# A list scheduler's clock for VectorE and GpSimd: one price more, and another order of layer 0

## The chip, the cores and the metric

The kernel runs on one core of a Trainium2 chip. The metric is the device time of one execution in microseconds (us); the median of several runs counts. The core has TensorE (PE; its weight loads are shown apart, as PEld), VectorE (DVE), ScalarE (ACT), GpSimd (POOL) and the DMA queues, of which SyncE (SP) issues most.

## The reference, cut to what matters

One inference step of a two-layer decoder, for a prompt of 256 tokens and 8 samples of one token (264 columns, T), all in float32:

```python
for i in range(DEPTH):                      # layer 0, layer 1
    h = rmsnorm(x, norm_mix[i])
    if i % 2 == 0:
        proj = h @ w_in_a[j]
        o_rwkv, sh, S = rwkv7_mix(proj[..., :RWKV_PROJ], ...)
        o_s5, hr, hi = s5_mix(proj[..., RWKV_PROJ:], ...)   # a scan over time, then y * sigmoid(y @ w_glu + b_glu)
        mix = jnp.concatenate([o_rwkv, o_s5], -1) @ w_out_a[j]
    else:
        proj = h @ w_in_c[j]
        mix, S = retention_mix(proj, st_ret[j], pos, ret_gn[j], w_out_c[j])
    x = x + mix.astype(x.dtype)
    h = rmsnorm(x, norm_ffn[i])
    x = x + swiglu(h, ffn_w_gate[i], ffn_w_up[i], ffn_w_down[i])
y = rmsnorm(x, norm_final)
```

Outputs are y of both groups and the final states of all mixers.

## The kernel before, in words

**The weight stream.** Every weight matrix is read in pieces of 512 rows by 256 columns (`raw`). A *granule* is half of one: 512 rows (4 tiles of 128) by 128 output columns. For each granule ScalarE rounds the weights to a short format (`wh`) and VectorE takes the rest (`wl<-raw,wh`, 128x512): `split_to` (L469), two granules ahead of their use. TensorE then does 12 matmuls, wh by xh, wh by xl and wl by xh for each of the 4 tiles. `run_stream` (L554) walks over all granules in a fixed order of tasks: the input projection of layer 0 (`w_in_a`, granules 0 to 135), the S5 gate (`s5_w_glu`, from granule 136), the output projection, the FFN, and the same for layer 1.

**The side work.** RWKV, S5, the samples and the evacuations of accumulators are generators whose operations are not issued at once but recorded (`issue`, L291) with what they depend on. Between two half granules `pump` (L518) issues recorded operations whose time, by the builder's own clocks, has come. A task that needs a flag (`need`, L549) forces side operations, earliest time first, until the flag is there: an input tile needs a free row buffer, the S5 gate needs the flag "s5".

**The clocks.** `emit` (L259) issues one instruction. It prices it with `cost` (L214), takes the larger of the engine's clock and the time its operands are ready (`after`, L241), and adds the price to the engine's clock `clk` ("P", "V", "S", "G", "D" for TensorE, VectorE, ScalarE, GpSimd and DMA). All choices, which recorded operation goes next and on which of two engines a copy or a square goes, are made by these clocks while the program is built. The finished program is a fixed order on each engine; on the chip the engines wait for each other by semaphores only. All instructions are issued through `emit`, so that nearly all have one line in the profile, L281 (L287 loads ScalarE's function tables).

**The chain of S5** (`s5`, L1145): GpSimd and VectorE prepare parameters, then a recurrence of 64 steps, each of three VectorE operations:

```python
            self.mul(t, bc(h[:, None], [128, 2, 2, 32]), w)
            self.add(o, o, t[:, 0])
            self.add(o, o, t[:, 1, ::-1])
```

In the profile these are `ar_tmp<-t,ar_tmp 128x128` and two `t<-t,ar_tmp 128x64`. After it comes `s5_out` (L1233), in two halves of eight rounds, one with its products on VectorE, one on GpSimd; each round's last matmuls and its copy `ar_tmp<-ps 128x164` wait for the recurrence. Then follow GELU (`128x1312`), a rearranging copy, and the flag "s5", behind which the gate's granules stand. The squares of the first norm (`first_squares`, L619) may go to ScalarE or GpSimd, their sums to VectorE or GpSimd.

Of the kernel before, what the change touches and what calls it, by code (L numbers as in the profile page):

```python
# [14 lines left out]
PSUM = bass.MemoryType.PSUM  # L15
# [45 lines left out]
class Task:  # L61
    def __init__(self, w, row0, nk, c0, rhs, done, need=None):
        self.w, self.row0, self.nk, self.c0 = w, row0, nk, c0
        self.rhs, self.done, self.need, self.pre = rhs, done, need, None
# [64 lines left out]
class Builder:  # L129
    def __init__(self, ctx, tc, ins, outs, dumps=None):  # L130
        self.ctx, self.tc, self.nc = ctx, tc, tc.nc
        self.I, self.O, self.C0 = ins, outs, ins["cst"]
        self.dumps = dumps or {}
        self.side, self.rec = [], None
        self.evac = Side(None, -1)
        self.clk = dict.fromkeys("PVSGD", 0.0)
        self.where, self.uses, self.pend = {}, {}, {}
        self.tick, self.cols, self.warm = 0, 0.0, False
        self.flags = Flags(self)
        self.act_set = None  # L140
        nc = self.nc
        self.V, self.G, self.S, self.P = (Eng(self, e, k) for e, k in
                                          ((nc.vector, "V"), (nc.gpsimd, "G"), (nc.scalar, "S"), (nc.tensor, "P")))
        self.Q, self.QG, self.QS = (Eng(self, e, "D") for e in (nc.sync, nc.gpsimd, nc.scalar))
        pool = lambda name, **k: ctx.enter_context(tc.tile_pool(name=name, **k))
        self.pw = pool("pw", bufs=1)
        self.pc = pool("pc", bufs=1)
        self.pb = pool("pb", bufs=1)
        self.ps = pool("ps", bufs=1, space=PSUM)
        ctx.enter_context(tc.manual_schedule())  # L150
        self.banks = [self.ps.tile([128, 512], F32, name=f"ps{i}", tag=f"ps{i}") for i in range(8)]
        self.layer, self.held = 0, {}
        self.turn, self.bank, self.open, self.busy = 0, {}, [], [None] * 4
        for b in self.banks:
            self.cells(b)
# [103 lines left out]
    def emit(self, eng, name, a, k):  # L259

        a = [self.real(x) for x in a]
        key, uses = eng.key, self.operands(name, a, k)
        c = self.cost(key, name, a)
        t = self.after(key, uses)
        if key == "D":
            one = a[1].ap[0][1] == 1 and a[0].shape[0] > 1
            t = self.clk["D"] = max(t + (7.5 if one else 1.7), self.clk["D"]) + c
        else:
            if key == "P":
                while self.clk["P"] + 0.1 >= (self.tick + 1) * 3.4133:  # L270
                    self.warm = self.cols >= 3277
                    self.tick, self.cols = self.tick + 1, 0.0
                n = int(np.prod(a[0].shape[1:]))
                self.cols += n * (1 if a[1].dtype == F32R else 2 if name == "transpose" else 4) * a[1].shape[0] / 128
                c *= 1 if self.warm else 2
            elif key == "S":
                self.functions(ACT_SET.get(a[2]))
            t = self.clk[key] = max(self.clk[key], t) + c
        for n, (at, bits), w in uses:
            self.uses[n][0 if w else 1, "PVSG".index(key) if key != "D" else 3][at] = t  # L280
        getattr(eng.eng, name)(*a, **k)  # L281
        return t
# [1546 lines left out]
```

## Time and profile before

| | |
|---|---|
| Median of 3 runs | 3126.82 us (3126.31 to 3127.84) |
| Profiled execution | 3128.85 us, span 3127.1 us |
| Granted TensorE clock, mean | 0.985 |
| Busy: PE, PEld, DVE, ACT, POOL | 3052.4, 2940.0, 1970.2, 1542.6, 333.9 us |
| Instructions of DVE, ACT, POOL | 3728, 2913, 527 |

The span is the time from the first to the last instruction of the profiled execution. A group of the profile is named by what it writes and reads (`wl<-raw,wh`) and its shape in partitions and elements. `ps` are the PSUM banks, `ar_...` the areas of layer 0, `t` the area that holds x and the S5 states. The records of two instructions in a row on one engine overlap by some 0.1 us.

### The profile page before, as it was taken

How to read it: one execution, taken by the hardware profiler on the slowest of the kernel's cores; microseconds unless marked ns; L12 is line 12 of the kernel's file. 1: busy time of each engine (PE TensorE's matmuls, PEld its weight loads, DVE VectorE, ACT ScalarE, POOL GpSimd, SP SyncE). 2: the span in 40 equal slices, each digit the busy share in tenths (PEclk: the TensorE clock that was granted, in tenths of full speed). 3: DMA queues.
4: the chain of work that ended last, by engine and by line, in shares of the span. 5: the costliest groups of instructions: out<-in, count | busy, mean ns of one | idle time of the engine just before them, and what ended most of it. 6: DMA issues, size and time to landing. Idle time of an engine off the chain costs nothing.

```text
span 3127.1 us, 66345 instructions
## 1 busy us (share of the span) xinstructions
PE 3052.4 (98%) x26510; PEld 2940.0 (94%) x26510; DVE 1970.2 (63%) x3728; ACT 1542.6 (49%) x2913; POOL 333.9 (11%) x527
## 2 busy tenths in 40 slices
PE   7999988999999999999999999999999999999998
PEld 7888777899999999999999999999999999999998
DVE  7779876565555556556566666566666555555554
ACT  5455456454444444455445444454455444444454
POOL 5012252110000000001111111011110000000001
PEclk9999899899999999999999999999999999999999
DMA  6235305465666666666777677577655666656664
GB/s 209 73 111 116 84 13 88 129 178 182 182 183 182 182 182 181 184 181 205 244 241 238 231 238 258 174 243 264 229 179 181 183 184 181 180 181 183 182 182 150
DMA packets 160614, 560.45 MB, mean 179 GB/s; under 512 B 21280, under 2 KB 23712, under 8 KB 160048
## 3 DMA queue, kind: packets, MB, share of 16 engines
q1 hardware_dynamic: 138960, 481.16, 50.4%
q0 software_dynamic: 20480, 73.44, 8.1%
q8 instruction: 208, 3.41, 0.4%
q10 hardware_dynamic: 864, 1.60, 0.1%
q14 instruction: 102, 0.84, 0.1%
HBM read 511.31 MB, written 42.69 MB: 177 GB/s over the span
## 4 chain that ended last, share of the span: by engine, by line
PE 90%; DVE 5%; ACT 2%; issue 1%; DMA 1%; POOL 1%; DVEq 0%; ACTq 0%; POOLq 0%
PE ps L281 90%; DVE ar_tmp L281 2%; DVE t L281 1%; DVE wl L281 1%; DMA sq<-ar_tmp 1%; ACT ar_tmp L281 1%; ACT wh L281 0%; DVE ar_hidx L281 0%; ACT sq L281 0%; DVE ar_hida L281 0%; POOL ar_tmp L281 0%; ACT L287 0%; DVE ar_hidb L281 0%; ACT ar_hidx L281 0%; DVE xl L281 0%
## 5 line engine op out<-in xcount | busy, mean ns | idle before, releaser
L281 DVE TENSOR_TENSOR wl<-raw,wh 128x512 fp32r<-128x512 f32 x1784 | 1256.0, 709 | 895.9 <-ACT wh L281 881.5
L281 ACT ACTIVATE wh<-raw 128x512 fp32r<-128x512 f32 x1784 | 1097.4, 627 | 914.7 <-PE ps L281 845.9
L281 PE MATMUL ps<-xh,wh 128*128 128x264 f32 x4512 | 1315.6, 292 | 14.6 <-ACT wh L281 12.8
L281 PE MATMUL ps<-xh,wl 128*128 128x264 f32 x4512 | 1285.8, 285 | 9.7 <-DVE wl L281 9.7
L281 PE MATMUL ps<-xl,wh 128*128 128x264 f32 x4512 | 1284.1, 285 | 0.0
L281 PEld LDWEIGHTS ps<-xh,wh 128*128 128x128 f32 x4512 | 854.8, 189 | 42.7 <-ACT wh L281 13.3
L281 PEld LDWEIGHTS ps<-xh,wl 128*128 128x128 f32 x4512 | 853.1, 189 | 11.5 <-DVE wl L281 11.5
L281 PEld LDWEIGHTS ps<-xl,wh 128*128 128x128 f32 x4512 | 855.7, 190 | 8.4 <-issue 4.8
L281 PE MATMUL ps<-hl,wh 128*128 128x264 f32 x1280 | 363.6, 284 | 0.0
L281 PE MATMUL ps<-hh,wh 128*128 128x264 f32 x1280 | 363.4, 284 | 0.0
L281 PE MATMUL ps<-hh,wl 128*128 128x264 f32 x1280 | 363.3, 284 | 0.0
L281 PE MATMUL ps<-n,wh 128*128 128x264 f32 x1408 | 257.0, 283 | 0.0
L281 PEld LDWEIGHTS ps<-hh,wh 128*128 128x128 f32 x1280 | 241.0, 188 | 0.0
L281 PEld LDWEIGHTS ps<-hh,wl 128*128 128x128 f32 x1280 | 240.8, 188 | 0.0
L281 PEld LDWEIGHTS ps<-hl,wh 128*128 128x128 f32 x1280 | 240.7, 188 | 0.0
L281 PE MATMUL ps<-ar_tmp 64*64 64x64 f32 (+7 forms) x2912 | 216.5, 285 | 16.6 <-DVE ar_tmp L281 11.8
L281 POOL TENSOR_TENSOR sqs<-sq,sqs 128x264 f32<-128x264 f32 x56 | 42.5, 759 | 1670.1 <-ACT sq L281 1670.1
L281 PEld LDWEIGHTS ps<-n,wh 128*128 128x128 f32 x1408 | 217.7, 188 | 0.0
L281 PEld LDWEIGHTS ps<-ar_tmp 64*64 64x64 f32 (+3 forms) x2912 | 149.9, 150 | 59.6 <-issue 26.0
L281 PE MATMUL ps<-n,wl 128*128 128x264 f32 x704 | 199.5, 283 | 0.0
L281 PE MATMUL ps<-omh,wh 128*128 128x264 f32 x512 | 146.1, 285 | 0.0
L281 PE MATMUL ps<-oml,wh 128*128 128x264 f32 x512 | 145.5, 284 | 0.0
(233 smaller groups left out, 2846.4 us busy)
## 6 DMA issues: line engine op xcount, KB each, us to landing
raw<-in_w_in_c_dram SPq DMA_DIRECT2D x192, 512.0 KB, 4.4
raw<-in_ffn_w_gate_dram SPq DMA_DIRECT2D x176, 512.0 KB, 3.7
raw<-in_ffn_w_up_dram SPq DMA_DIRECT2D x176, 512.0 KB, 3.7
raw<-in_ffn_w_down_dram SPq DMA_DIRECT2D x176, 512.0 KB, 3.6
out_dram<-ar_tmp POOLq DMA_DIRECT2D x72, 512.0 KB, 4.6
raw<-in_w_in_a_dram SPq DMA_DIRECT2D x68, 512.0 KB, 3.8
ar_tmp<-in_state_ret_dram POOLq DMA_DIRECT2D x64, 512.0 KB, 6.7
raw<-in_w_out_c_dram SPq DMA_DIRECT2D x64, 512.0 KB, 4.0
```

What stands on the lines that cost most here:

```text
L281: getattr(eng.eng, name)(*a, **k)
```

## The change

Two flags, `slow["V"]` and `slow["G"]`, say whether the last operation put on VectorE and on GpSimd had all its operands outside PSUM. When such an operation is put on one of the two, starts (by the clocks) before the other's clock, and the other's last one was such an operation too, its price rises by a share of the overlap, at most of its own price: 0.9 on VectorE, 0.2 on GpSimd. Nothing else is changed: the same operations are issued, with the same operands.

```diff
@@ -134,6 +134,7 @@
         self.clk = dict.fromkeys("PVSGD", 0.0)
+        self.slow = dict(V=False, G=False)
         self.where, self.uses, self.pend = {}, {}, {}
@@ -275,7 +276,16 @@
                 self.functions(ACT_SET.get(a[2]))
-            t = self.clk[key] = max(self.clk[key], t) + c
+            t = max(self.clk[key], t)
+            if key in "VG":
+                other = "GV"["VG".index(key)]
+                if not any(str(x.space) == str(PSUM) for x in a if hasattr(x, "space")):
+                    if t < self.clk[other] and self.slow[other]:
+                        c += min(c, self.clk[other] - t) * (0.9 if key == "V" else 0.2)
+                    self.slow[key] = True
+                else:
+                    self.slow[key] = False
+            t = self.clk[key] = t + c
         for n, (at, bits), w in uses:
```

The line of nearly all instructions moves from L281 to L291. The order changes in layer 0 throughout, and in a few places of layer 1. Two places follow.

VectorE, in the forced stretch at granule 113 (split 116), where the recurrence's steps (`ar_tmp<-t_77,ar_tmp 128x128` and `t_77<-t_77,ar_tmp 128x64`) stand among RWKV's operations (`ar_hida`, `ar_hidx`, and those that read `ps`). Before:

```order
L281 TENSOR_TENSOR wl<-raw,wh 128x512
L281 TENSOR_TENSOR ar_tmp<-t_77,ar_tmp 128x128
L281 TENSOR_TENSOR ar_tmp<-ps_69,cst 128x256
L281 TENSOR_TENSOR t_77<-t_77,ar_tmp 128x64
L281 SCALAR_TENSOR_TENSOR ar_hidx<-ar_hida,pcol,ar_hidx 128x256
L281 TENSOR_TENSOR t_77<-t_77,ar_tmp 128x64
L281 TENSOR_TENSOR ar_hida<-ar_hidx,ar_hida 128x4x64
L281 TENSOR_TENSOR ar_tmp<-t_77,ar_tmp 128x128
L281 TENSOR_TENSOR ar_hida<-t_77,ar_hida 128x4x64
```

Now:

```order
L291 SCALAR_TENSOR_TENSOR ar_hida<-ar_hida,pcol,ar_hidx 128x256
L291 TENSOR_TENSOR ar_tmp<-t_77,ar_tmp 128x128
L291 TENSOR_TENSOR ar_tmp<-ps_71,cst 128x256
L291 TENSOR_TENSOR t_77<-t_77,ar_tmp 128x64 x2
L291 TENSOR_TENSOR ar_tmp<-t_77,ar_tmp 128x128
L291 TENSOR_TENSOR t_77<-t_77,ar_tmp 128x64 x2
L291 TENSOR_TENSOR ar_tmp<-t_77,ar_tmp 128x128
L291 TENSOR_TENSOR t_77<-t_77,ar_tmp 128x64
```

Steps of the recurrence now stand back to back in this stretch: 14 of them begin between split 116 and split 117, where 6 did before; RWKV's `ar_hidx` and `ar_hida` come later in it.

VectorE, at the last step of the recurrence and the first products of `s5_out` (`ar_tmp<-ar_tmp 128x160`). Before, with the last step just behind split 136:

```order
L281 TENSOR_TENSOR wl<-raw,wh 128x512
L281 TENSOR_TENSOR ar_tmp<-t_77,ar_tmp 128x128
L281 TENSOR_TENSOR ar_hidb<-ar_hidy 64x4x64
L281 TENSOR_TENSOR t_77<-t_77,ar_tmp 128x64
L281 TENSOR_TENSOR ar_hidb<-ar_hidy 64x4x64
L281 TENSOR_TENSOR wl<-raw,wh 128x512
L281 TENSOR_TENSOR t_77<-t_77,ar_tmp 128x64
L281 TENSOR_TENSOR ar_tmp<-ar_tmp 128x160 x2
```

Now, with the last step behind split 132 and split 133 after it:

```order
L291 TENSOR_TENSOR ar_tmp<-t_77,ar_tmp 128x128
L291 SCALAR_TENSOR_TENSOR t_77<-t_77,pcol,ar_hidx 128x256
L291 TENSOR_TENSOR t_77<-t_77,ar_tmp 128x64
L291 SCALAR_TENSOR_TENSOR ar_hidb<-ps_72,ar_hidb 128x256
L291 TENSOR_TENSOR t_77<-t_77,ar_tmp 128x64
L291 TENSOR_TENSOR wl<-raw,wh 128x512
L291 TENSOR_TENSOR ar_tmp<-ar_tmp 128x160 x2
```

The recurrence ends four splits earlier in VectorE's queue, and four splits that stood ahead of its last step stand behind it.

## Rows read from the trace of the kernel before

**Rows 1.** The page, busy us and share of the span, instructions of each engine.

```profile
PE 3052.4 (98%) x26510; PEld 2940.0 (94%) x26510; DVE 1970.2 (63%) x3728; ACT 1542.6 (49%) x2913; POOL 333.9 (11%) x527
```

**Rows 2.** Stretches of 160 us: length, then busy us and instructions of each engine.

```profile
core 0: us, PE busy (x) PEld busy (x) DVE busy (x) ACT busy (x) POOL busy (x), PEclk, DMA share, GB/s
...
160.00:320.00 160.00, 148.50 (x1386) 137.09 (x1382) 131.74 (x355) 88.80 (x204) 33.56 (x62) 0.94 0.50 114
320.00:480.00 160.00, 141.42 (x1788) 119.18 (x1789) 128.85 (x369) 80.82 (x214) 56.45 (x102) 0.90 0.22 53
480.00:640.00 160.00, 147.04 (x1687) 129.70 (x1684) 93.98 (x223) 81.34 (x197) 27.03 (x36) 0.92 0.53 110
...
800.00:960.00 160.00, 160.00 (x1326) 160.00 (x1325) 94.98 (x166) 76.98 (x138) 0.00 (x0) 1.00 0.62 183
```

**Rows 3.** PE's waits at 0:120, 240:340, 340:480 us: total, times, longest.

```profile
PE ps L281 <- DVE wl L281: 7.1, 5, 2.4
...
PE ps L281 <- DVE ar_tmp L281: 4.7, 5, 1.5
...
PE ps L281 <- DVE ar_tmp L281: 11.4, 15, 1.4
```

**Rows 4.** Three stretches of layer 0, columns as in rows 2.

```profile
256.50:379.00 122.50, 111.69 (x1291) 98.04 (x1290) 108.38 (x311) 63.06 (x162) 35.05 (x59) 0.90 0.52 97
379.00:485.30 106.30, 91.69 (x1161) 75.76 (x1160) 81.31 (x234) 57.51 (x156) 42.52 (x76) 0.86 0.11 33
...
6.80:28.40 21.60, 13.14 (x86) 12.20 (x87) 21.58 (x27) 12.83 (x28) 17.58 (x20) 1.00 0.70 267
```

**Rows 5.** DVE's timeline: start, us, what it does.

```profile
15.96 2.26 DVE L281 TENSOR_TENSOR wl<-raw,wh 128x512 fp32r<-128x512 f32 x2
...
255.47 0.38 DVE L281 TENSOR_TENSOR ar_tmp<-t,ar_tmp 128x128 f32<-128x128 f32 x1
...
270.38 0.70 DVE L281 TENSOR_TENSOR wl<-raw,wh 128x512 fp32r<-128x512 f32 x1
...
275.91 1.10 DVE L281 TENSOR_TENSOR ar_tmp<-t,ar_tmp 128x128 f32<-128x128 f32 x1
...
378.98 0.38 DVE L281 TENSOR_TENSOR ar_tmp<-t,ar_tmp 128x128 f32<-128x128 f32 x1
```

**Rows 6.** POOL's timeline in the prologue and beside the fourth row of rows 5.

```profile
5.56 0.63 POOL L281 TENSOR_TENSOR rstd<-t 128x264 f32<-128x264 f32 x1
...
16.60 1.07 POOL L281 TENSOR_TENSOR sqs<-sqs,sq 128x264 f32<-128x264 f32 x1
...
275.56 1.28 POOL L281 TENSOR_TENSOR ar_tmp<-ar_tmp 128x512 f32<-128x512 f32 x1 [0.76 <-DVE ar_tmp L281]
```

**Rows 7.** DVE's groups from 200 to 390 us: busy us, mean ns, idle before.

```profile
L281 DVE TENSOR_TENSOR wl<-raw,wh 128x512 fp32r<-128x512 f32 x63 | 45.0, 720 | 15.1 <-ACT wh L281 14.8 <-issue 0.2
L281 DVE TENSOR_TENSOR t<-t,ar_tmp 128x64 f32<-128x64 f32 x128 | 39.9, 312 | 1.0
...
L281 DVE TENSOR_TENSOR ar_tmp<-ps,cst 128x256 f32<-128x256 f32 x14 | 5.8, 415 | 1.6 <-PE ps L281 1.5
```

**Rows 8.** Chain of waits (one row), then timelines, from 379 to 485 us.

```profile
382.75 14.67 PE ps L281 x138
...
458.57 0.30 ACT L281 ACTIVATE ar_tmp<-ps 128x164 f32<-128x164 f32 x1
...
468.97 2.48 ACT L281 ACTIVATE ar_tmp<-ar_tmp 128x1312 f32<-128x1312 f32 x2
...
484.26 0.59 PE L281 MATMUL ps<-xh,wh 128*128 128x264 f32 x1
```

**Rows 9.** Stretches of 6 us at granule 113, columns as in rows 2.

```profile
280.00:286.00 6.00, 2.39 (x40) 1.96 (x39) 6.00 (x18) 2.78 (x10) 2.52 (x3) 0.84 0.82 198
286.00:292.00 6.00, 6.00 (x46) 4.84 (x45) 5.81 (x16) 2.32 (x4) 2.87 (x5) 0.50 0.76 93
292.00:298.00 6.00, 6.00 (x62) 5.29 (x62) 3.23 (x11) 3.06 (x10) 0.00 (x0) 0.53 0.90 48
```

## The prediction

> **What bounds the kernel now.** I read the page's busy shares first, then the span cut into stretches of 160 us, then the waits of TensorE, then VectorE's timeline in the stretches where TensorE waits. The shares say TensorE: 98% of the span [rows 1]. The stretches say where the other 2% is: from 640 us on TensorE is busy for all of every stretch at the full granted clock, 2.4 GHz (one of fifteen such rows up to 3040 us is shown), so nothing that the list does there can save or cost time unless it makes a wait of its own. From 160 to 640 us the clock is 0.90 to 0.94 and the weight loads are busy for 119 to 137 of 160 us [rows 2]. This is layer 0, whose many small operations the list places between the weight matmuls. There TensorE waits for VectorE: 7.1 us for `wl` splits in the first 120 us, 4.7 us for side results from 240 to 340 us, 11.4 us from 340 to 480 us [rows 3]. VectorE itself is busy for 108.38 of 122.50 us between 256.5 and 379 us, and for 81.31 of 106.30 us in the stretch after it [rows 4]. So VectorE's queue in layer 0 is what this change can move; any gain is a part of the 43 us in which TensorE is not busy between 160 and 640 us (480 less 148.50, 141.42 and 147.04 [rows 2]), and of the time at the lower clock.
>
> **The price that the list now counts.** The trace shows that what is priced is real. A split `wl` takes 0.70 us by itself; two of them, in the prologue beside GpSimd, take 2.26 us, 1.13 each; a recurrence product of 128x128 takes 0.38 us alone and 1.10 us beside a GpSimd product of 1.28 us [rows 5, 6]. The new price (0.9 of the list's own price at most) fits the long operation: `cost` has 0.60 us for it, so up to 0.54 more, and the trace shows 0.43 more. For the short one, 0.20 us in `cost`, it gives 0.18 more, and the trace shows 0.72. The Trainium skill, in "SBUF — State Buffer", section "Who interferes with whom", has a stricter rule: a VectorE operation with two SBUF inputs and a GpSimd operation that reads SBUF exclude each other, and the second to issue waits until the first is through. By that rule the 128x128 product would wait for the rest of the GpSimd one, an estimate of 0.93 us (275.56 + 1.28 - 275.91); the trace agrees roughly, with 0.72. By it the list would still run ahead of VectorE at every short operation, and the sum below would shrink to nearly nothing (rival B).
>
> **The change, term by term.** No arithmetic is added or removed; each engine gets the same work in another order, but for two squares that go from GpSimd to ScalarE and one sum each way between VectorE and GpSimd. So only the order can pay.
>
> 1. *The end of the S5 recurrence (64 steps on VectorE).* This is the largest shift. Before, 754 VectorE instructions stand ahead of its last step, now 738. Four of the 16 are `wl` splits (136 ahead before, 132 now), the other twelve net are side operations, mostly of 128x256. At 720 ns a split and 415 ns for the commonest 128x256 form [rows 7] that is 4 x 0.72 + 12 x 0.415 = 7.9 us less VectorE work before the recurrence ends. VectorE is busy 88% of the time there [rows 4], so the end, at 379.0 us now [rows 5], should come about 7.9 us sooner. What hangs on it: `s5_out` may finish its eight rounds only after the recurrence; its last output copy starts at 458.57 us, the two GELUs at 468.97 us, and the first gate matmul that needs them at 484.26 us [rows 8]. From the recurrence's end to that matmul no weight matmul can run ahead. What was moved behind the end must be done somewhere: VectorE is idle for 106.30 - 81.31 = 25 us in that stretch [rows 4], room for the twelve side operations (5.0 us). The four splits (2.9 us) are needed at once by the last weight matmuls of the input projection and stand before the first round of `s5_out`; half of them, 1.4 us, I count as given back, since the GpSimd half of `s5_out` goes on beside them. Net -6.5 us.
> 2. *The prologue.* VectorE is busy for 21.58 of 21.60 us from 6.8 us on [rows 4], and TensorE waits for its splits. Two squares leave GpSimd, whose such operations take 0.63 us alone and up to 1.07 beside VectorE [rows 6]. Bounds: 0 (the port was free), and 2 x 0.85 = 1.7 us gained if all of GpSimd's time was VectorE's loss. Half of that, 0.85, less one sum of 264 columns that VectorE gets, some 0.42 us by the 256 columns of [rows 7]: -0.4 us.
> 3. *The forced stretch at granule 113*, where an input-projection tile waits for a free row buffer. 571 instead of 551 VectorE instructions stand ahead of split 117, the balance of eight more steps of the recurrence (24 instructions) and fewer of RWKV. At 312 ns for the commonest form [rows 7] that is 20 x 0.312 = 6.2 us by which the next weight matmuls may start later. I count 0, since the recurrence, and not these 23 granules, sets when the gate matmuls begin; without that cover it costs the 6.2 us (rival C).
> 4. *The queues.* SP issues the same loads, a weight load or two earlier or later among the small ones; GpSimd's three row-spreading DMAs move by a place or two. None of the waits read names a DMA [rows 3]: 0. One issue that came late on GpSimd behind a product would cost up to that product's 1.28 us [rows 6], which I keep for the range.
> 5. *Layer 1* changes in a few places, under a TensorE that is busy without a gap [rows 2]: 0.
>
> Sum: -6.5 - 0.4 = -6.9 us. The profiled execution took 3128.85 us, which gives 3121.95; the median of the three runs is 2.03 us below the profiled one, so the forecast for the median is **3120 us**, 0.22% faster. About 0.2%, or 6.3 us, is what a measurement can tell from no change; the forecast lies right there.
>
> **The rivals.**
>
> *B: nothing arrives, 3126.* The order moves but VectorE's total work up to the gate matmuls is the same, so what leaves the front of the recurrence comes back behind it. For it: VectorE is the busiest side engine on both sides of the recurrence's end, and in the stretch behind it the chain of waits runs over TensorE for 14.67 us at a stretch [rows 8]. By the skill's rule above the new price is also a quarter of the real one for the recurrence's steps, so that the list would not be nearer to the chip where it matters. Against it: 25 us of idle VectorE behind the end. This is also the case in which the change doesn't do what it says. Only the 0.4 us of the prologue stay: 3126.4, say 3126, within 3121 to 3131.
>
> *C: the weight matmuls become the late ones, 3135.* Split 117 and all behind it come 6.2 us later, and the granules 113 to 136 with them. TensorE was busy for 2.39 of 6 us just before, and the granted clock then stood at about 0.5, the lower of its two levels (1.2 GHz), for the 12 us that followed, with TensorE busy throughout [rows 9]. A longer idle stretch there leaves more of its work at the lower level: for a quarter as long again, 3 us, it is 1.5 us (an estimate from these rows). It decides if the last of these granules ends after the recurrence would have let `s5_out` through: 3126.8 + 6.2 + 1.5 = 3134.5, say 3135. For it: the order rows. Against it: in the stretch up to 379 us the recurrence ends last now.
>
> **How the numbers follow.** Forecast case A has 0.62; its own range is 3110 to 3126, since 7.9 / 0.88 = 9 us and the 1.7 us of the prologue could arrive whole, and a stretch at the lower clock of 12 us [rows 9] could vanish (6 us): 16.7 in all. I put 0.43 of it beyond 0.2% and 0.19 within. B has 0.18 (0.15 within, 0.01 faster, 0.02 slower), C 0.20 (0.17 slower, 0.03 within). Together: faster 0.44, same 0.37, slower 0.19. The range of 3110 to 3135 holds A, B and most of C.
>
> **What would show it.** The last 128x128 step of the recurrence near 371 instead of 379 us, the first gate matmul near 478 instead of 484 us, and VectorE busy for more of that stretch: term 1 is right. If the step comes earlier but the gate matmul does not, it is B. If split 117 starts after 300 us (294.9 now) and the recurrence still ends at 379, it is C. I am wrong altogether if the two profiles differ after 640 us, or if the difference sits before 240 us.

## The result, and the profile after

| | before | changed |
|---|---|---|
| Median of 3 runs | 3126.82 us (3126.31 to 3127.84) | 3145.36 us (3145.19 to 3148.60) |
| Profiled execution | 3128.85 us, span 3127.1 us | 3145.19 us, span 3143.4 us |
| Ratio of the times, 95% interval | 1 | 1.0054 [1.0036, 1.0072] |

The changed kernel is slower, by 17 us by this ratio (the two medians are 18.5 us apart); 3120 was forecast, and the range ended at 3135. The page's first part shows the same work as [rows 1], two squares moved as the order said:

```profile
PE 3054.0 (97%) x26510; PEld 2942.4 (94%) x26510; DVE 1969.1 (63%) x3728; ACT 1544.2 (49%) x2915; POOL 336.7 (11%) x525
```

The stretches of 160 us, columns as in [rows 2], show where: TensorE is busy 9 us less from 160 to 320 us and 8 us less from 480 to 640 us. At 800 us nothing differs, and the `wl` splits from the 171st to the end all start 14.4 to 18.9 us later than before (16.4 us at the 174th and 175th), so that the whole loss arises ahead of the 171st, which started at 612 us.

```profile
160.00:320.00 160.00, 139.32 (x1234) 127.71 (x1233) 125.65 (x343) 82.31 (x185) 31.58 (x58) 0.91 0.46 111
320.00:480.00 160.00, 143.56 (x1807) 122.76 (x1807) 122.31 (x352) 72.77 (x215) 51.98 (x95) 0.88 0.25 51
480.00:640.00 160.00, 138.96 (x1762) 120.32 (x1762) 100.19 (x242) 88.42 (x205) 36.11 (x48) 0.94 0.50 103
800.00:960.00 160.00, 160.00 (x1326) 160.00 (x1325) 94.79 (x167) 76.77 (x138) 0.00 (x0) 1.00 0.61 182
```

Stretches of equal length compare different work once one kernel is late. So I cut both at the same splits (splits are counted from 1, granules from 0): from split 113 to split 139, the last one issued ahead of the wait for the flag "s5", and from there to split 140, the first one behind it. Splits 137 to 139 hold weights of the gate already, since splits run two granules ahead. Before:

```profile
276.94:385.88 108.94, 96.87 (x1146) 84.16 (x1144) 95.39 (x268) 50.92 (x131) 28.49 (x47) 0.88 0.50 88
385.88:488.75 102.87, 90.41 (x1196) 74.48 (x1196) 77.90 (x231) 60.36 (x162) 42.87 (x77) 0.86 0.09 29
```

After:

```profile
276.30:418.40 142.10, 112.49 (x1342) 98.10 (x1340) 111.79 (x314) 62.07 (x169) 42.84 (x70) 0.83 0.41 73
418.40:506.94 88.54, 76.49 (x886) 61.56 (x887) 67.08 (x191) 54.07 (x139) 35.32 (x61) 0.81 0.10 31
```

Two things are to be seen. More side work stands in the first part (VectorE 111.79 against 95.39 us) and less in the second, which is 14 us shorter. And TensorE's idle time in the first part went from 108.94 - 96.87 = 12.1 to 142.10 - 112.49 = 29.6 us. These 17.5 us are about as large as the loss. The waits of TensorE from 276 to 420 us (total, times, longest) name what came in. Before:

```profile
PE ps L281 <- DVE ar_tmp L281: 8.1, 11, 1.5
...
PE ps L281 <- POOL ar_tmp L281: 1.0, 1, 1.0
```

After:

```profile
PE ps L291 <- POOL ar_tmp L291: 12.9, 3, 5.6
PE ps L291 <- DVE ar_tmp L291: 8.0, 5, 5.4
PE ps L291 <- DVE ar_hida L291: 4.6, 1, 4.6
```

GpSimd's 12.9 us, in three waits, were 1.0 us before. The timelines of the changed kernel from 317 to 363 us (start, us; in brackets the idle time before and its releaser) show what stands behind them:

```profile
317.17 0.53 POOL L291 DMA_DIRECT2D sq<-ar_tmp  x1 [0.29 <-POOL ar_tmp L291]
...
329.97 0.55 POOL L291 DMA_DIRECT2D sq<-ar_tmp  x1
...
336.41 2.02 ACT L291 ACTIVATE sq<-sq,ar_tmp 128x64 f32<-128x64 f32 x8 [7.38 <-DMA sq<-ar_tmp]
...
338.56 1.28 POOL L291 TENSOR_TENSOR ar_tmp<-ar_tmp,sq 128x512 f32<-128x512 f32 x1 [3.24 <-ACT sq L291]
...
338.98 1.40 DVE L291 TENSOR_TENSOR wl<-raw,wh 128x512 fp32r<-128x512 f32 x1 [5.13 <-ACT wh L291]
...
362.40 1.02 PE L291 MATMUL ps<-ar_tmp 128*64 128x2 f32 x16 [5.63 <-POOL ar_tmp L291]
```

This is a round of the sample (`rwkv_sample_half`). A row of 512 numbers is spread over 64 partitions, once for each half of the partitions (`spread`: two DMAs on GpSimd's queue), ScalarE scales it in eight operations, GpSimd adds it to the state, and TensorE multiplies the state. ScalarE stands 7.38 us at the scalings, with the roundings `wh` behind them in its queue; VectorE's `wl` waits for those; and TensorE waits at the sample's own small matmuls, with weight matmuls behind them (the last row is the next round). The two DMAs of one spread are issued 12.8 us apart, and the scaling waits for the second.

ScalarE's waits for these DMAs from 0 to 620 us (first row) are 27.3 us before and 44.1 after. From 276 us to split 139 alone (second row) they are 9.2 and 28.2 us, and VectorE's waits for `wh`, from split 113 to the last step of the recurrence (third row), are 6.8 and 19.6 us:

```profile
ACT sq L281 <- DMA sq<-ar_tmp: 27.3, 5, 7.1
...
ACT sq L281 <- DMA sq<-ar_tmp: 9.2, 2, 6.9
...
DVE wl L281 <- ACT wh L281: 6.8, 7, 2.1
```

```profile
ACT sq L291 <- DMA sq<-ar_tmp: 44.1, 8, 10.2
...
ACT sq L291 <- DMA sq<-ar_tmp: 28.2, 4, 10.2
...
DVE wl L291 <- ACT wh L291: 19.6, 7, 5.6
```

The rows that the prediction had asked for, from the timelines of VectorE, ScalarE and TensorE: the last 128x128 step of the recurrence, the GELUs and the gate matmul, 8.3, 17.3 and 18.3 us later than in [rows 5, 8]. That matmul is the seventh of the gate's first granule, not the first as the prediction has it; the first starts at 480.71 us before and at 497.69 now, 17.0 us later.

```profile
387.29 0.38 DVE L291 TENSOR_TENSOR ar_tmp<-t,ar_tmp 128x128 f32<-128x128 f32 x1
...
486.24 2.48 ACT L291 ACTIVATE ar_tmp<-ar_tmp 128x1312 f32<-128x1312 f32 x2
...
502.60 0.59 PE L291 MATMUL ps<-xh,wh 128*128 128x264 f32 x1
```

### The profile page after: what moved, and what is told of

Read it like the earlier page. It is cut to its first block, busy times and chain, and to the rows that moved or that the text cites. A ratio compares the mean times of both kernels' runs of the same rounds, so it can differ in the third digit from the quotient of the medians.

```text
span 3143.4 us, 66318 instructions
## 1 busy us (share of the span) xinstructions
PE 3054.0 (97%) x26510; PEld 2942.4 (94%) x26510; DVE 1969.1 (63%) x3728; ACT 1544.2 (49%) x2915; POOL 336.7 (11%) x525
## 3 DMA queue, kind: packets, MB, share of 16 engines
q8 instruction: 208, 3.41, 0.5%
## 4 chain that ended last, share of the span: by engine, by line
PE 91%; DVE 3%; ACT 2%; DMA 2%; issue 1%; POOL 0%; DVEq 0%; ACTq 0%; SPq 0%; POOLq 0%
PE ps L291 91%; DVE ar_tmp L291 2%; DMA sq<-ar_tmp 1%; ACT ar_tmp L291 1%; DVE t L291 1%; DVE wl L291 1%; ACT wh L291 0%; ACT sq L291 0%; POOL ar_tmp L291 0%; DVE ar_hida L291 0%; ACT L297 0%; DVE ar_hidx L291 0%; DVE ar_hidb L291 0%; DMA ar_tmp<-in_s5h_dram 0%; ACT ar_hidx L291 0%
## 5 line engine op out<-in xcount | busy, mean ns | idle before, releaser
L291 DVE TENSOR_TENSOR wl<-raw,wh 128x512 fp32r<-128x512 f32 x1784 | 1258.8, 710 | 926.4 <-ACT wh L291 911.2
L291 ACT ACTIVATE wh<-raw 128x512 fp32r<-128x512 f32 x1784 | 1098.3, 628 | 917.7 <-PE ps L291 855.4
L291 PE MATMUL ps<-xh,wh 128*128 128x264 f32 x4512 | 1316.6, 292 | 20.3 <-ACT wh L291 11.4
L291 PE MATMUL ps<-xh,wl 128*128 128x264 f32 x4512 | 1284.6, 285 | 3.5 <-DVE wl L291 3.5
L291 PE MATMUL ps<-xl,wh 128*128 128x264 f32 x4512 | 1283.6, 284 | 0.0
L291 PEld LDWEIGHTS ps<-xh,wh 128*128 128x128 f32 x4512 | 854.2, 189 | 50.4 <-issue 14.0
L291 PEld LDWEIGHTS ps<-xl,wh 128*128 128x128 f32 x4512 | 855.1, 190 | 9.0 <-issue 5.5
L291 PEld LDWEIGHTS ps<-xh,wl 128*128 128x128 f32 x4512 | 852.3, 189 | 4.7 <-DVE wl L291 4.5
L291 PE MATMUL ps<-hl,wh 128*128 128x264 f32 x1280 | 363.6, 284 | 0.0
L291 PE MATMUL ps<-hh,wh 128*128 128x264 f32 x1280 | 363.4, 284 | 0.0
L291 PE MATMUL ps<-hh,wl 128*128 128x264 f32 x1280 | 363.3, 284 | 0.0
L291 PE MATMUL ps<-n,wh 128*128 128x264 f32 x1408 | 257.0, 283 | 0.0
L291 PE MATMUL ps<-ar_tmp 64*64 64x64 f32 (+8 forms) x2912 | 214.8, 282 | 29.8 <-DVE ar_tmp L291 14.7
L291 PEld LDWEIGHTS ps<-hh,wh 128*128 128x128 f32 x1280 | 241.0, 188 | 0.0
L291 PEld LDWEIGHTS ps<-hh,wl 128*128 128x128 f32 x1280 | 240.8, 188 | 0.0
L291 PEld LDWEIGHTS ps<-hl,wh 128*128 128x128 f32 x1280 | 240.7, 188 | 0.0
L291 POOL TENSOR_TENSOR sqs<-sq,sqs 128x264 f32<-128x264 f32 x56 | 43.4, 775 | 1665.0 <-ACT sq L291 1665.0
L291 PEld LDWEIGHTS ps<-n,wh 128*128 128x128 f32 x1408 | 217.7, 188 | 0.0
L291 PEld LDWEIGHTS ps<-ar_tmp 64*64 64x64 f32 (+3 forms) x2912 | 148.1, 147 | 67.6 <-issue 22.7
L291 PE MATMUL ps<-n,wl 128*128 128x264 f32 x704 | 199.5, 283 | 0.0
L291 PE MATMUL ps<-omh,wh 128*128 128x264 f32 x512 | 145.9, 285 | 0.3 <-DVE t L291 0.2
L291 PE MATMUL ps<-oml,wh 128*128 128x264 f32 x512 | 145.5, 284 | 0.0
```

## The experiments

Ratios are to the kernel before on the same chip, with 95% intervals; 0.001 is 3.1 us.

**Scalings later on ScalarE (e1, e2).** While the program is written out, a row scaling is kept back and issued behind the second next `wh`, or ahead of its reader if that comes first. The list's clocks and all other queues stay as they were.

```diff
+        if key == "S" and name == "activation" and hasattr(self, "vrow") and a[0].tensor is self.vrow.tensor and ...
+            self.late.append([2, eng, name, a, k, uses])
+            return t
+        if any((w or ow) and n == m and b & c for l in self.late for n, (_, b), w in uses for m, (_, c), ow in l[5]):
+            self.settle(True)
         getattr(eng.eng, name)(*a, **k)
+        if key == "S" and ... and a[0].tensor.name.startswith("wh"):
+            self.settle(False)
```

> The changed kernel, every queue in its own order, except that on ScalarE the sample's eight row scalings (sq<-sq,ar_tmp 128x64) are issued up to two weight roundings (wh) later, never behind their reader. Theory T (ScalarE stands at these scalings waiting for the row-spreading DMA, with the next wh behind it, and so VectorE's wl and TensorE): the TensorE gaps near 309, 335 and 357 us (5.4 + 4.8 + 5.6 us) go, and part of the half-clock time behind them: 3125 to 3132. Rival V (the new order puts VectorE work ahead of the splits, the waits on ScalarE are only where that shows): 3142 to 3146, the gaps stay with another releaser. Rival E (the loss comes from granules 46 to 58): 3145.

> Control: the same move of the row scalings in the kernel before. There one such wait of 2.3 us stands in the forced stretch. Theory T: 3123 to 3127, since only that one can go. Rival V: 3127. If it loses as much as e1 wins, the move acts by something else than these waits.

e1 measured 1.0025 [1.0015, 1.0035], e2 0.9975 [0.9963, 0.9987]. About half of the loss went, and the kernel before gained as well, more than either theory had: about 8 us in both. Of e2's gain, the splits up to 139 show nothing (385.8 us against 385.9); it comes from split 150 on, in the second half of the sample. In e1 split 139 starts at 412.4 us, 6.0 sooner than in the changed kernel. So ScalarE's queue at these scalings costs time in both kernels, and ahead of split 139 in the changed one alone; but by the times of the whole the move is worth the same in both.

**The price in a part of the program (e3 to e6).** `run_stream` notes the granule `gi`, and the price is counted only in a part of them.

```diff
-                    if t < self.clk[other] and self.slow[other]:
+                    if self.gi < 80 and t < self.clk[other] and self.slow[other]:
```

> The new price is counted only up to granule 79, so that the order from granule 80 on is nearly that of the kernel before (two ScalarE rounds move by one place), while granules 46 to 58 keep the changed order. Theory T: 3127 plus or minus 3, the time lies in the forced stretch at granule 113. Rival E (granules 46 to 58 lose 5 us and a stretch at the lower clock): 3132 to 3136. Rival N (any other order of the same work costs about as much): 3130 to 3145.

> The new price is counted only from granule 113 on, where the kernel before waits for a free row buffer: the order up to there is that of the kernel before, the forced stretch is again longer (8.9 us on the list's own clock; 4.6 before, 12.3 in the changed kernel), and two rounds of row scalings again stand ahead of wh 117. Theory T: most of the loss, 3136 to 3146, with ScalarE waiting over 5 us for the spreading DMA. Rival E: 3127. Rival V: 3140 to 3146, since 611 VectorE instructions stand ahead of granule 117 (610 in the changed kernel, 586 before).

> The new price is counted from granule 100 on. At granule 113 the list then stands as in the changed kernel (513 VectorE and 2000 TensorE instructions issued, 518 and 2009 in the kernel before) and forces 12.3 us of side work by its own clock (changed 12.3, e4 8.9, before 4.6). Theory T2 (what counts is how far the side work has come when granule 113 begins to wait; the longer the forced stretch, the longer TensorE has nothing): 3136 to 3146. Rival P (the price itself puts the layer in a better order, as e4 suggests, and the loss is made ahead of granule 100): 3122 to 3128.

> The new price is counted up to granule 112, the mirror image of e4: the list comes to granule 113 exactly as in the changed kernel and forces 11.4 us there, then goes on without the price. Theory T2: 3138 to 3148, since the state at granule 113 is the changed kernel's. Rival Q (the order behind granule 113 is what the price spoils): 3129 to 3134. If e4 and e6 add up (-4 and +17 make +13), the parts are independent; if not, the greedy order reacts to any push.

| price counted | ratio | VectorE side instructions ahead of split 139 | start of split 139, us | of split 140 |
|---|---|---|---|---|
| nowhere (before) | 1 | 635 | 385.9 | 488.8 |
| up to granule 79 (e3) | 1.0017 [1.0003, 1.0031] | 636 | 388.6 | 484.1 |
| from 113 (e4) | 0.9982 [0.9972, 0.9991] | 621 | 385.0 | 483.5 |
| from 100 (e5) | 1.0022 [1.0009, 1.0034] | 656 | 406.1 | 493.6 |
| everywhere (changed) | 1.0054 [1.0036, 1.0072] | 673 | 418.4 | 506.9 |
| up to 112 (e6) | 1.0083 [1.0070, 1.0095] | 767 | 471.5 | 533.6 |

e4 is a miss for theory T and rival V alike: the price alone, behind granule 113, made the kernel a little faster; E, with no loss, was nearest. By the times the two parts add up within their intervals (e4 and e6 together +0.65%, the whole +0.54%), by the start of split 139 they do not (0.9 us sooner and 85.6 later, the whole 32.5 later). T2 is not borne out: by its ratio e5 lies between T2's range and P's, and e6 above T2's. The profile of e5 is its fastest run (3124.91 us, median 3137.91), so that its two starts are those of a fast execution.

e3 is slower by about 5 us (1 to 10), within the ranges of E and N and above T's. Its split 113 starts 4.9 us later than before (281.9 against 276.9). That of the changed kernel, whose price goes on, does not (276.3, and 277.8 in e11): it has the same early granules and makes up for them between splits 65 and 113. So e3's 5 us are not shown to be a part of the change's loss.

**A fifth of the price (e7).**

```diff
-                        c += min(c, self.clk[other] - t) * (0.9 if key == "V" else 0.2)
+                        c += min(c, self.clk[other] - t) * (0.2 if key == "V" else 0.05)
```

> About a fifth of the price (0.2 and 0.05 in place of 0.9 and 0.2). If the effect goes with the price: 3128 to 3132. Rival N (a small push moves the greedy list to another order, and the order of the kernel before is simply a good one): not between; the forced stretch is 9.3 us on the list's clock, 25 VectorE instructions more than before stand ahead of granule 117's state, and the list's own clock has the S5 flag at 403.6 us (before 390.2, changed 397.5): 3138 to 3150.

1.0051 [1.0038, 1.0064]: a fifth of the price costs as much as all of it. The loss does not go with the size of the price. A small push sends the list, which always takes the earliest operation, into another order (724 side instructions ahead of split 139, with the whole price 673).

**e4 with the scalings of e1 (e8).**

> e4 with the move of e1 and e2: price from granule 113 on, and ScalarE's row scalings up to two weight roundings later. If the two gains are separate (-4 to -6 and -7): 3115 to 3121, under both kernels. If both remove the same waits: 3122 to 3126.

Both edits, no other line: 0.9968 [0.9956, 0.9981], 3118.98 us. The gains of e4 and e2 add up within the intervals, and this version beats both kernels.

**The forced stretch (e9 to e12).** What the list forces at granule 113 and the awaited flag does not need is kept back and issued behind split 117.

```diff
+        if self.holding and self.cur is not None and self.cur not in self.rwkv:
+            self.held_ops.append((eng, name, a, k, uses))
+            return t
```

> The changed kernel in its own order, but of the work that the list forces at granule 113, what the awaited flag does not need (recurrence steps, a sample round with its GpSimd and ScalarE operations) is issued behind split 117: 556 in place of 572 VectorE instructions ahead of it, 30 in place of 36 recurrence steps, and the second round of row scalings behind wh 117. Theory F (the forced stretch itself costs: TensorE has nothing while VectorE and ScalarE work through what the flag does not need): 3135 to 3141 if the changed kernel stands at 3145. Rival R (the recurrence sets the end, so pushing its steps back costs what the splits win): 3144 to 3149.

> e9 and e1 together in the changed kernel. Theory F: under e1 (ratio 1.0025), 3131 to 3136; what is then left over the kernel before, 4 to 6 us, is what granules 46 to 58 lose (e3, 1.0017). Rival R: like e1, 3138 to 3141.

> The changed kernel again, beside e9, e10 and e12 on one chip: 3143 to 3149, ratio 1.004 to 1.007 by the first measurement. If it comes out under 1.003, what e1, e9 and e10 won has to be counted against that.

> e8 (price from granule 113 on, row scalings later; ratio 0.9968) with the forced work of granule 113 behind split 117 (555 in place of 568 VectorE instructions ahead of it). Theory F: 3112 to 3118. Rival R: 3119 to 3124, no gain over e8.

e11 measured 1.0049 [1.0033, 1.0065], e9 1.0062 [1.0049, 1.0076], e10 1.0045 [1.0032, 1.0058], e12 0.9990 [0.9979, 1.0000]. Theory F falls: split 117 came 5.2 us sooner in e9 than in e11 (309.0 against 314.2 us), the recurrence ended 2.1 us later (390.2 against 388.1) and split 139 too (421.3 against 419.2). TensorE's idle time only moved: ahead of the matmuls of granule 113 it fell from 11.4 us in e11 to 4.6 in e9, and from there to split 139 it rose from 17.2 to 26.7. e12 and e10 are slower than e8 and e1, with intervals that hardly overlap; by their ratios e9, e10 and e12 lie in rival R's ranges.

**How much side work stands ahead of split 139 (e13 to e16).** In the table above the ratios rise with that count, by and large. The sample's generator now waits for a granule, an edit that has nothing to do with the price; `run_stream` sets the flag at granule 126 (e13, e14), 118 (e15) or 136 (e16).

```diff
     def rwkv_sample(self):
+        yield from self.wait("later")
```

> The changed kernel, the sample's generator may start only from granule 126 on. 602 side instructions of VectorE then stand ahead of split 139 (673 without the edit, 635 in the kernel before). Theory N (that number sets when the last input-projection granules end, some 0.2 us of the whole per instruction by e3 to e7): ratio 0.995 to 0.999. Rival W (only ScalarE's waits and granules 46 to 58 count; no sample, no waits ahead of granule 126): 1.0015 to 1.003. Rival O (the order is a matter of luck): up to 1.006.

> The same edit in the kernel before: here the list answers with more side work ahead of split 139, 743 instead of 635. Theory N: 1.005 to 1.009, the opposite sign of e13 from the same edit. Rival W: 0.996 to 1.000, since the waits for the spreading DMA go here too.

> The kernel before with the sample from granule 118 on: 646 ahead of split 139. Theory N: 1.0005 to 1.003. Rival W: 0.997 to 1.000.

> e4 (price from granule 113 on) with the sample from granule 136 on: 698 ahead of split 139 (e4: 621). Theory N: 1.003 to 1.006. Rival W: 0.995 to 0.998, as e8.

Measured: e13 1.0078 [1.0059, 1.0096], e14 1.0035 [1.0023, 1.0047], e15 1.0029 [1.0016, 1.0042], e16 0.9977 [0.9967, 0.9988]. e13 has the wrong sign, and e16 too; e14 is below theory N's range, and e15 alone lies in it. Rival W is right for e16 alone, and e13 is above rival O's 1.006. The start of split 139 goes with the count, by and large (14.5 us sooner than before with 602, 52.1 later with 743, 3.6 sooner with 646, 19.5 later with 698), but the end does not. The stretches of e13, from split 113 to 139 and from there to 140, show why:

```profile
281.24:371.38 90.14, 84.37 (x1025) 73.76 (x1023) 79.96 (x255) 37.71 (x80) 14.12 (x27) 0.91 0.32 88
371.38:516.50 145.12, 118.92 (x1087) 96.26 (x1088) 91.23 (x249) 73.24 (x220) 59.35 (x98) 0.65 0.30 37
```

What leaves the first part comes into the second, ahead of the gate's flag, and there the granted clock was 0.65 (0.86 before) and TensorE was idle for 26.2 us (12.5 before): 145 us where the kernel before has 103. Theory N is wrong as a cause of the time.

**The two DMAs of a spread together (e17, e18).** The list gives DMAs one clock. `emit` sets it to the time at which a DMA has landed (7.5 us are counted for one of one partition), and `choices` offers the next DMA only from then on. So the second half of a spread is held back until, by the list's clock, the first has landed, and on the chip it then stands behind whatever GpSimd was given meanwhile. Here the second is issued right behind the first, in the last three of the four spreads of each half of the sample; nothing else is moved, and VectorE, ScalarE and TensorE keep their orders (`twin` holds, for each DMA of a spread, which half it is and the operands of both).

```diff
+        if key == "D" and id(a[1]) in self.twin:
+            if self.twin[id(a[1])][0]:
+                return t
+            for h in range(2):
+                eng.eng.dma_start(*self.twin[id(a[1])][1][h])
+            return t
```

> The changed kernel, every queue in its own order, but the two DMAs of a spread (rounds 1 to 3 of each half) are issued one right behind the other. Theory D (the late second DMA holds ScalarE, GpSimd and, through the sample's own matmuls, TensorE): ScalarE's waits for it fall from 44 to under 20 us, the TensorE gaps near 309, 335 and 357 us (15.8 us together) nearly go, TensorE's idle time between splits 113 and 139 falls from 29.6 to 14 to 20 us, and the ratio from 1.005 to 0.998 to 1.002, better than e1. Rival W (only the queue order on ScalarE counts, as e1): 1.002 to 1.003. Rival S (the rest of the order is the cause): over 1.003.

> The same in the kernel before, where the second DMA is issued 2.8 to 11.2 us after the first and ScalarE waits 27 us for it in layer 0 (2.3 and 6.9 us of it ahead of split 139). Theory D: 0.995 to 0.998, by less than in the changed kernel. If it gains as much as e17, the late DMA is not what the change made worse.

e17 measured 0.9983 [0.9973, 0.9994], 3122.21 us; e18 0.9953 [0.9937, 0.9968], 3116.47 us, the lowest median of all. Theory D holds in both, but for the 22.2 us below, over the 20 it allowed, and an idle time of 20.1 us, at the end of its range; W and S fall. e17, stretches as above, then timelines, then waits: ScalarE's from 0 to 620 us, VectorE's from split 113 to the last step of the recurrence, TensorE's from 276 to 420 us:

```profile
277.04:404.24 127.20, 107.09 (x1342) 93.05 (x1340) 112.37 (x313) 62.20 (x169) 43.02 (x70) 0.89 0.48 81
404.24:492.82 88.58, 76.34 (x882) 61.74 (x882) 66.97 (x190) 54.04 (x139) 35.11 (x61) 0.81 0.10 31
```

```profile
314.73 1.10 POOL L296 DMA_DIRECT2D sq<-ar_tmp  x2 [0.29 <-POOL ar_tmp L298]
...
327.93 2.00 ACT L298 ACTIVATE sq<-sq,ar_tmp 128x64 f32<-128x64 f32 x8
```

```profile
ACT sq L298 <- DMA sq<-ar_tmp: 22.2, 5, 5.4
...
DVE wl L298 <- ACT wh L298: 5.2, 5, 1.4
...
PE ps L298 <- POOL ar_tmp L298: 4.2, 3, 2.5
```

With the same 112 us of VectorE work, the first part is 15 us shorter, TensorE's idle time in it 20.1 instead of 29.6 us, and this round's scaling, at 336.41 with a wait of 7.38 us in the changed kernel, comes at 327.93 without any. VectorE's waits for `wh` are down from 19.6 to 5.2 us, and TensorE's for GpSimd from 12.9 to 4.2. In e18 the first part is only 3.9 us shorter than before, since only one long wait stood there, and the rest of the gain is in the sample's second half:

```profile
277.32:382.33 105.01, 93.61 (x1146) 81.29 (x1144) 95.44 (x267) 50.93 (x131) 28.58 (x47) 0.91 0.52 91
382.33:485.78 103.45, 90.26 (x1187) 75.09 (x1188) 78.30 (x231) 60.25 (x162) 43.07 (x77) 0.86 0.09 28
```

How much of the change's loss this is: e17 gains 0.0066 on e11, e18 gains 0.0047, so that most of the gain would be had without the change. The two kernels stood 0.0049 apart in e11, and with the DMAs together 0.9983 - 0.9953 = 0.0030. So by the times the late DMA makes some 0.002 (6 us) of the loss, with an uncertainty of 0.0025 from the three intervals: it is not clear of nothing, and most of the loss is not explained by it. The traces show more of it ahead of split 140: there e17 is 14.1 us ahead of the changed kernel (492.8 against 506.9) and e18 3.0 ahead of the kernel before (485.8 against 488.8), so that 11 of the 18 us by which the change is late at that place go with the DMAs; behind it e18 gains more than e17 does. These are single profiles, and the two of the changed kernel differ by 0.7 us at split 140 and by 3.3 at split 171.

What is left, 0.0030, was not isolated. In the traces of e17 and e18 it shows in the start of split 139 (404.2 against 382.3 us), of which a part is made good behind it (split 140 at 492.8 against 485.8), and it stands mainly at the forced stretch. From the first matmul of granule 112 to that of granule 113, TensorE is idle for 20.42 - 9.45 = 11.0 us in e17 and for 7.01 - 3.41 = 3.6 us in e18, of 20.1 and 11.4 us between splits 113 and 139:

```profile
279.69:300.11 20.42, 9.45 (x101) 7.47 (x99) 16.00 (x40) 7.14 (x22) 8.07 (x13) 0.65 0.60 68
```

```profile
279.43:286.44 7.01, 3.41 (x48) 2.98 (x47) 7.01 (x22) 3.48 (x11) 2.52 (x3) 0.95 0.85 175
```

e9 shortened this stretch and won nothing, but with the DMAs still apart. No run has both edits, so that the forced stretch stays open as the cause of the rest.

## Why the prediction was wrong

**Term 1, the recurrence.** The step that failed is that 7.9 us less VectorE work, with VectorE busy 88% of the time, should bring the end "about 7.9 us sooner". The work did shrink (89.7 us busy from split 113 to the last step before, 85.0 after); the idle time was taken as fixed, and it was not. In that stretch VectorE was idle 12.4 us before and 25.9 after, since `wl` now stood waiting for `wh`, 19.6 us instead of 6.8, and the recurrence stood behind `wl`. It ended 8.3 us later. e17 shows the term without that wait: idle 10.5 us, last step at 373.2 us, 5.8 sooner than before. Against e18 (376.2 us), where the same wait is gone from the order before, it is 3.1 us: the direction of the work term was right, less than half of its size is seen, and the idle time was left out.

**What hangs on it.** "From the recurrence's end to that matmul no weight matmul can run ahead" also failed. In the changed kernel splits 133 to 139 come behind the recurrence, and split 139 is 32.5 us later than before. In e17 the recurrence ends 5.8 us sooner and split 140 still starts 4.1 us later. Counting 1.4 us for the splits that had moved behind was the error: they became the late ones, as in rival C, and 17.8 of the 32.5 us are there at split 117 already.

**Term 2, the prologue.** Split 41 starts 1.9 us sooner; 0.4 was forecast within 0 to 1.7 us. But the order of granules 42 to 60 had no term at all: split 49 starts 14.3 us sooner, split 57 9.5 later, split 65 5.1 later. The difference is gone at split 113 (-0.6 us), so that leaving it out did no harm here; that was luck, since in e3, with the price up to granule 79 alone, split 113 starts 4.9 us later.

**Term 3, granule 113.** Split 117 came 17.8 us later; 6.2 were worked out from 20 more VectorE instructions (with seven more steps of the recurrence among them, 36 against 29, and not eight). Between splits 113 and 117 VectorE was busy for 10.0 us more (26.48 against 16.47) and idle for 8.5 us more (9.92 against 1.47), 5.01 of it for `wh` right ahead of split 117. TensorE was idle 10.6 us ahead of the matmuls of granule 113 (3.6 before). That this counts for nothing in the end is not shown: e9 won nothing by a shorter stretch, but in e17 TensorE is still idle 11.0 us there, and these are most of the idle time that it has more than e18.

**Term 4, the queues.** "None of the waits read names a DMA", and so 0, is the step whose failure stands behind that of term 1. The waits read were TensorE's alone. ScalarE's waits in the same trace name the spreading DMA five times, 27.3 us in layer 0, and ScalarE stands ahead of VectorE's splits. The order also showed that GpSimd's DMAs moved; "by a place or two" was put at 1.28 us at most. In the four spreads ahead of split 139 the second DMA came 2.8 to 11.2 us behind the first before (7.0 on average), and 8.3 to 12.8 us in the changed kernel (10.4). With the two together (e17), TensorE's idle time between splits 113 and 139 fell by 9.5 us, and the time of the whole by 0.0066 against e11.

**Term 5 and the rivals.** Layer 1 gave nothing, as said. B was wrong: the recurrence did not come sooner. C had the sign and the splits, though not its own sign of the recurrence still ending at 379 us, and stopped at 3135 because it counted work and a little of the clock but no wait. The 12 us at the lower clock at granule 113 [rows 9] did not vanish either: the granted clock from split 113 to 139 was 0.83, against 0.88 before.

## What to carry to other kernels

When a change reorders in-order queues, count the work ahead of a step, but also read the waits of every engine that the step's engine waits for, here ScalarE behind a DMA: what hung on the late DMAs (15 us in the kernel before, 21 in the changed one, by e18 and e17) was more than all the work counted (7.9 us). A list scheduler with a more faithful price need not give a better order; test such a price at a fifth of its size and in parts of the program before explaining its sign. And a clock that runs to a transfer's landing must not also decide when the next transfer may be issued.

## What the runs showed of the hardware

The recurrence's 128x128 product, VectorE's groups from 0 to 620 us (busy us, mean ns, idle before), got longer under an order made to keep VectorE and GpSimd apart, from 430 to 469 ns (460 to 476 in e11 and e17, with the same order on VectorE); single ones took up to 1.36 us (1.17 before), and the split above, beside a GpSimd sum, 1.40 instead of 0.70:

```profile
L281 DVE TENSOR_TENSOR ar_tmp<-t,ar_tmp 128x128 f32<-128x128 f32 x64 | 27.5, 430 | 0.5
```

```profile
L291 DVE TENSOR_TENSOR ar_tmp<-t,ar_tmp 128x128 f32<-128x128 f32 x64 | 30.0, 469 | 0.7
...
282.81 1.36 DVE L291 TENSOR_TENSOR ar_tmp<-t,ar_tmp 128x128 f32<-128x128 f32 x1
```

The spreading DMA of 128 KB, from one partition to 64, takes 6.4 us from issue to landing (median of eight, first row, changed kernel). Two in a row do not overlap fully: of the pair in e17 that is issued from 314.73 us on (next two rows), the first takes 7.0 us and the second 10.9, each from its own issue.

```profile
sq<-ar_tmp POOLq DMA_DIRECT2D x8, 128.0 KB, 6.4
```

```profile
sq<-ar_tmp POOLq DMA_DIRECT2D x1, 128.0 KB, 7.0
...
sq<-ar_tmp POOLq DMA_DIRECT2D x1, 128.0 KB, 10.9
```

The Trainium skill, in "DMA: Bandwidth & Descriptors", section "Anatomy of one DMA", fits the time of a DMA on GpSimd's path as 2.0 us and the bytes at 436 GB/s. By it this one would take 2.3 us (an estimate from that page); the trace does not agree, 6.4 us, and the list's own 7.5 is the nearer figure.
